# The low part of 33 weights: from a VectorE subtraction to a ScalarE negation and an adding transfer

## The chip, the core and the metric

One core of a Trainium2 chip runs the whole program. The metric is device time of one execution in microseconds. Engines are named as in the profile: PE (TensorE matmul), PEld (TensorE weight load), DVE (VectorE), ACT (ScalarE), POOL (GpSimd), SP (SyncE, which here only starts transfers).

## The reference, cut to what matters

Two blocks run one after the other on 256 latent tokens of width 1024; the first also has 256 context tokens. The first block has two layers. Each modulates its tokens, multiplies them by one wide weight matrix, and goes on in three branches: attention, a gated linear recurrence, and a spatial gating unit. Cut to the two branches that matter here:

```
h = x * (1 + scale) + shift                       # context tokens likewise
q, k, v, gates, ... = split(h @ w_in)
q, k = rope(rms_norm(q)), rope(rms_norm(k))       # 8 heads of 64, 2 key/value heads
y_attn = softmax(q @ k_all.T / 8) @ v_all * silu(a_g)
vn = layer_norm(s_v)                              # spatial gating, width 512, chunks of 128
y_sgu = s_u * (w_s @ vn + b_s) * silu(s_g)
```

In layer 0 all 512 tokens are computed; in layer 1 only the 256 latent ones need queries and gating, while keys and values are made for all 512. The second block (a gated delta rule and a convolution) isn't touched by the change.

## The kernel before, in words

All weights lie in one array W of pieces, each 128 partitions by 1024 float32 (512 KB). A product is made in three matmuls of a faster 32-bit type (F32R): each operand is split into a high part (the operand rounded to F32R) and a low part (the operand less its high part), and high x high, high x low and low x high are summed (`mm3`, L220, and `gemm_mv`, L294). A float32 product of 128 rows and up to 512 columns is thus three matmuls.

`weight` (L237) brings one piece: `raw` (L232) starts the load on SP's queue into one of three buffers tagged "raw"; then, under `urgent` (a higher place in the order of the work), `split` (L212) makes the high part `wh` with an ACT cast (L214) and the low part `wl` with a DVE subtraction (L215). `wh` and `wl` have three buffers each, so a weight can be split only when the weight three before it has been used up. The tile framework sets the order of each engine's instructions when the program is built, by priority and by the time at which it expects operands to be ready; on the chip each engine keeps to its order.

Two ways of using a weight matter here. In `gemm_mv` the weights are the moving operand, 256 columns: a pair of pieces covers the 1024 rows of the contraction, and for each tile of 128 tokens 4 steps use the first piece and then 4 steps the second, 24 matmuls per tile; a pair serves 4 tiles in layer 0 (96 matmuls) and 2 in layer 1's queries and gating values (48). In `gemm_st` (L273) one piece is the stationary operand of 8 steps, 24 matmuls of 512 columns in layer 0 and of 256 in layer 1.

`trunk` (L487) runs a layer: `attention` (L661) and then `sgu` (L553) first, each wholly, then the recurrence with the rest of the products between its steps. In layer 0 `attention` uses one piece of 512 columns (the last of four for key, value and half of the queries; the first three were used in `start`, L384) and a pair for the other queries; in layer 1 a pair for key and value and two for the queries. `sgu` uses two pairs for the values, and through `gemm_st` 4 pieces for the units (L580) and, in `gate_y` (L601), 4 for the gate. Attention's own work (softmax: DVE maxima L780, ACT exponentials L781, PE transposes and products) is laid by the framework between the products of `sgu`.

POOL's queue in this part of the program holds small loads for attention and gating (L558, L560, L666), the loads of modulation weights of `ada_sums` (L443), each of which waits for a DVE accumulation (L449) that frees its buffer, and at the start of layer 1 products on POOL itself (L1130, L1131).

Of the kernel before, what the change touches and what calls it, by code (L numbers as in the profile page):

```python
# [8 lines left out]
F32 = mybir.dt.float32  # L9
# [4 lines left out]
ALU = mybir.AluOpType  # L14
# [88 lines left out]
INDEX = {k: i for i, k in enumerate(PLAN)}  # L103
# [77 lines left out]
class Builder:  # L181
    def __init__(self, nc, tc, io):
        self.nc, self.tc, self.io = nc, tc, io
        self.n = 0
        self.hold = {}

    def nm(self, s):
        self.n += 1
        return f"{s}_{self.n}"
# [47 lines left out]
    def weight(self, key, pool=None, name="", calm=False):  # L237

        hold = self.hold.pop(key, ())
        with nullcontext(), self.behind(*hold):  # L240
            raw = self.raw(key)
        with self.urgent(), self.behind(*hold):
            h = self.t(pool or self.wpool, [P, 1024], F32R, tag="wh" + name)
            l = self.t(pool or self.wpool, [P, 1024], F32R, tag="wl" + name)
            self.split(h, l, raw)
        return h, l

    def rstd(self, pool, out, x, n):
# [238 lines left out]
    def trunk(self, l):  # L487
        nc, tc, io = self.nc, self.tc, self.io
        self.T0, self.TN = (0, 512) if l == 0 else (256, 256)
        self.tiles = [0, 1, 2, 3] if l == 0 else [2, 3]  # L490
        TN = self.TN
        with tc.tile_pool(name=f"m{l}", bufs=1) as mp:
            self.mp = mp
            if l == 0:
                self.yraw_a = self.big([P, 4, TN], tag="ya")
                self.yraw_g = self.big([P, 4, TN], tag="yg")
                self.m = [self.big([P, 4, TN], tag=f"m{i}") for i in range(2)]
            else:
                m = self.big([P, 8, TN], tag="m0")
                self.m = [m[:, 0:4], m[:, 4:8]]  # L500
                y = self.big([P, 8, TN], tag="m1")
                self.yraw_a, self.yraw_g = y[:, 0:4], y[:, 4:8]
            self.decay = self.decay_inputs(l)
            next(self.decay, None)
            with tc.tile_pool(name=f"sgu{l}", bufs=1) as sp:
                self.attention(l)
                self.sgu(l, sp)
            self.tgp = mp
            units = self.units(l)
            pre0, rate0, mid, rate1 = PACES[l]  # L510
            for n, rate, hp in ((pre0, rate0, 0), (mid, rate1, 1)):
                for _ in range(int(n)):
                    next(units, None)
                due = 0.0
                for _ in self.gla(l, hp):
                    due += rate
                    while due >= 1:
                        due -= 1
                        next(units, None)
                if l == 0 and hp == 0:  # L520
                    with tc.tile_pool(name="ada", bufs=2, side="right", reuse_waits="tile") as raws:
                        self.adaln(mp, raws)
                    self.tgp = tc.alloc_tile_pool(name="tg", bufs=1, side="right", reuse_waits="tile")
            for _ in units:
                pass
            if l == 0:
                self.g0 = self.big([P, 2, D])
                self.g1 = self.big([P, D], tag="ya")
                self.ada_gate(self.grow, [self.g0[:, 0], self.g0[:, 1], self.g1])
            for _ in self.gate_y(l, G_G, self.yraw_g):  # L530
                pass
            with tc.tile_pool(name=f"late{l}", bufs=1, reuse_waits="tile") as lp:
                self.lp = lp
                self.mh = self.t(lp, [P, 8, TN], F32R, tag="mh")
                self.ml = self.t(lp, [P, 8, TN], F32R, tag="ml")
                for _ in self.branch(l, "bg", M_G, 2, tg=self.tg):
                    pass
                if l:
                    self.out_ln(l)
                else:  # L540
                    self.tgp.release()
                    with tc.tile_pool(name="ln", bufs=1, reuse_waits="tile") as self.lp:
                        self.out_ln(l)
# [1359 lines left out]
```

## Time and profile before

| what | value |
|---|---|
| median of 3 runs | 1443.71 us (1441.45 to 1444.53) |
| the profiled execution's own time | 1437.33 us |
| its span, first to last instruction | 1435.6 us |
| layer 0's attention and gating | from about 49 to about 200 us of the span |
| layer 1's attention and gating | from about 595 to about 710 us of the span |
| mean DMA rate over the span | 131 GB/s |

The span and the rows below are of one profiled execution. A row of the view by stretch gives for each engine its busy time and, in brackets, its instructions, then the granted PE clock as a share of full speed, the mean busy share of the core's 16 DMA engines and their rate. In the views by instruction a bracket at the end tells how long the engine was idle before it and what ended that.

### The profile page before, as it was taken

To read this page: it belongs to the slowest core of one execution; us is meant where nothing else is said; L and a number is where in the kernel's file an instruction comes from. 1 tells how busy PE (TensorE), PEld (TensorE's weight loads), DVE (VectorE), ACT (ScalarE), POOL (GpSimd) and SP (SyncE) were. 2 spreads that over 40 slices of the span, in tenths; PEclk is the share of its full clock that TensorE was granted. 3 is DMA by queue.
4 is the path that set the end of the run, shared out by engine and by line. 5 is a ranking of instruction groups with operands and counts; after the bars stand their busy time and mean duration, and the time that the engine had idled before them with its cause. 6 is when DMAs were issued, how large, how long until landed. Compare 5 with 4: busy or idle time off the path is not lost.

```text
span 1435.6 us, 31593 instructions
## 1 busy us (share of the span) xinstructions
PE 1357.7 (95%) x13036; PEld 1199.8 (84%) x13036; DVE 1065.3 (74%) x2034; ACT 831.3 (58%) x1490; POOL 88.9 (6%) x260
## 2 busy tenths in 40 slices
PE   7899999999999999899999998979899999999998
PEld 4796778777877779896899988979789998989997
DVE  2598742898888268878639468877998776899785
ACT  2445533752455334656667485479685557877654
POOL 0100000111101000300001001011000000100000
PEclk9999999999999999999999999989999999999999
DMA  9442122335632236352233344424333553423362
GB/s 382 164 132 91 34 74 89 103 105 170 229 116 75 74 110 202 105 178 76 91 129 130 125 133 162 171 88 135 104 114 124 176 163 118 133 92 120 117 208 86
DMA packets 52848, 187.56 MB, mean 131 GB/s; under 512 B 6136, under 2 KB 7468, under 8 KB 52704
## 3 DMA queue, kind: packets, MB, share of 16 engines
q1 hardware_dynamic: 44640, 159.90, 33.0%
q0 software_dynamic: 6912, 24.39, 5.1%
q8 instruction: 102, 1.67, 0.5%
q10 hardware_dynamic: 1152, 1.25, 0.3%
q14 instruction: 42, 0.34, 0.1%
HBM read 184.47 MB, written 1.05 MB: 129 GB/s over the span
## 4 chain that ended last, share of the span: by engine, by line
PE 59%; DVE 15%; ACT 11%; DMA 8%; issue 5%; POOL 1%; ACTq 0%; SPq 0%; DVEq 0%; POOLq 0%
PE pg L218 47%; PE px L218 5%; DVE wl L215 4%; DMA adaw<-in_W 3%; PE px L227 3%; ACT wh L214 3%; DVE u L1761 3%; DMA raw<-in_W 2%; PE px L804 1%; DMA araw<-in_W 1%; DVE acc L449 1%; DMA xT<-in_xT 1%; DVE hTl L215 1%; PE px L987 1%; PE px L954 1%
## 5 line engine op out<-in xcount | busy, mean ns | idle before, releaser
L215 DVE TENSOR_TENSOR wl<-raw,wh 128x1024 fp32r<-128x1024 f32 x276 | 336.9, 1224 | 173.3 <-ACT wh L214 163.5
L214 ACT CAST wh<-raw 128x1024 fp32r<-128x1024 f32 (+1 forms) x278 | 289.0, 1043 | 291.6 <-PE pg L218 239.6
L218 PE MATMUL pg<-hTh,wh 128*128 128x256 f32 (+1 forms) x1440 | 454.9, 316 | 0.6 <-ACT wh L214 0.4
L218 PE MATMUL pg<-hTl,wh 128*128 128x256 f32 (+1 forms) x1440 | 449.5, 313 | 2.6 <-DVE ss L718 1.4
L218 PE MATMUL pg<-hTh,wl 128*128 128x256 f32 (+1 forms) x1424 | 444.4, 312 | 0.9 <-DVE wl L215 0.8
L218 PEld LDWEIGHTS pg<-hTl,wh 128*128 128x128 f32 x1440 | 270.6, 188 | 21.0 <-issue 5.5
L218 PEld LDWEIGHTS pg<-hTh,wh 128*128 128x128 f32 x1440 | 270.8, 188 | 20.5 <-issue 3.0
L218 PEld LDWEIGHTS pg<-hTh,wl 128*128 128x128 f32 x1424 | 268.5, 189 | 16.7 <-issue 1.4
L1761 DVE SCALAR_TENSOR_TENSOR u<-cpad,cols,u 128x256 f32<-128x256 f32 x240 | 104.8, 482 | 0.9
L218 PE MATMUL pg<-big,wh 128*128 128x512 f32 (+1 forms) x384 | 99.3, 347 | 5.5 <-DVE th L612 3.0
L218 PE MATMUL pg<-wl,hTh 128*128 128x256 f32 x320 | 91.2, 285 | 1.9 <-DVE wl L215 1.9
L218 PE MATMUL pg<-wh,hTh 128*128 128x256 f32 x320 | 91.7, 287 | 0.6 <-ACT kd L855 0.6
L218 PE MATMUL pg<-wh,hTl 128*128 128x256 f32 x320 | 91.0, 284 | 0.0
L218 PEld LDWEIGHTS pg<-big,wh 128*128 128x128 f32 x384 | 66.5, 193 | 15.5 <-DVE th L612 3.6
L218 PE MATMUL pg<-wh,mh 128*128 128x256 f32 x272 | 76.8, 284 | 0.5 <-DVE y L1320 0.5
L218 PE MATMUL pg<-wl,mh 128*128 128x256 f32 x272 | 76.7, 283 | 0.5 <-DVE wl L215 0.5
L218 PE MATMUL pg<-wh,ml 128*128 128x256 f32 x272 | 76.7, 282 | 0.0
L449 DVE SCALAR_TENSOR_TENSOR acc<-adaw,sc,acc 128x1024 f32<-128x1024 f32 x49 | 62.2, 1281 | 16.0 <-DMA adaw<-in_W 15.9
L218 PE MATMUL pg<-big,wl 128*128 128x512 f32 (+1 forms) x192 | 66.2, 346 | 0.0
L218 PEld LDWEIGHTS pg<-wl,hTh 128*128 128x128 f32 x320 | 61.1, 191 | 2.5 <-DVE wl L215 2.1
L218 PEld LDWEIGHTS pg<-wh,hTh 128*128 128x128 f32 x320 | 61.2, 191 | 1.6 <-ACT kd L855 1.0
L218 PEld LDWEIGHTS pg<-wh,hTl 128*128 128x128 f32 x320 | 61.3, 191 | 0.1
(451 smaller groups left out, 2440.4 us busy)
## 6 DMA issues: line engine op xcount, KB each, us to landing
raw<-in_W SPq DMA_DIRECT2D x282, 512.0 KB, 3.4
adaw<-in_W POOLq DMA_DIRECT2D x32, 512.0 KB, 3.6
araw<-in_W SPq DMA_DIRECT2D x16, 512.0 KB, 9.0
xT<-in_xT SPq DMA_DIRECT2D x4, 512.0 KB, 9.5
yg<-in_xtok POOLq DMA_DIRECT2D x2, 512.0 KB, 4.3
m<-in_xtok POOLq DMA_DIRECT2D x2, 512.0 KB, 5.3
nwrow<-in_nwrow POOLq DMA_DIRECT2D x2, 512.0 KB, 3.7
wsT<-in_sguw POOLq DMA_DIRECT2D x2, 256.0 KB, 3.7
```

The lines of the kernel that those rows point to most:

```text
L214: self.nc.scalar.copy(h, src)
L215: self.nc.vector.tensor_tensor(l, src, h.bitcast(F32), ALU.subtract)
L218: self.last_mm = self.nc.tensor.matmul(out, lhsT, rhs, start=start, stop=stop).ins
L227: self.nc.tensor.transpose(out, in_, self.ident[:k, :k])
L449: nc.vector.scalar_tensor_tensor(acc[:, v], raw, sc, acc[:, v], ALU.mult, ALU.add)
L804: nc.tensor.matmul(pv[64 * j:64 * j + 64, :256], kv[kt][:, 128 + 64 * g:192 + 64 * g], pTs[b][:, j * 256:(j + 1) * 256], start=kt == 0, st ...
L954: nc.tensor.matmul(out[o, a, :], x[:, a, o], y[:, a, o], start=True, stop=True, tile_position=(0, 32 * b))
L987: nc.tensor.matmul(pa[ks, a, ts], e[ch, li, a, ks], qe[ch, li, a, ts], start=True, stop=True, tile_position=(64 * d, s0))
L1761: nc.vector.scalar_tensor_tensor(out, src, w, out, ALU.mult, ALU.add)
```

## The change

A flag, `relief`, is on while `attention` and `sgu` of each layer are laid out. While it is on, `weight` makes the low part in another way: ACT casts the high part as before; ACT then writes its negative into the low part's tile; and a second transfer of the same piece of W, started by POOL (`gpsimd.dma_start` with an adding `accum_op`), adds the weight itself, so that the tile holds weight less high part. The DVE subtraction falls away for these weights. The raw load on SP's queue stays, and its buffer is now read by the cast alone.

```diff
@@ -183,6 +183,7 @@
         self.nc, self.tc, self.io = nc, tc, io
         self.n = 0
         self.hold = {}
+        self.relief = False
 
     def nm(self, s):
         self.n += 1
@@ -242,7 +243,13 @@
         with self.urgent(), self.behind(*hold):
             h = self.t(pool or self.wpool, [P, 1024], F32R, tag="wh" + name)
             l = self.t(pool or self.wpool, [P, 1024], F32R, tag="wl" + name)
-            self.split(h, l, raw)
+            if self.relief:
+
+                self.nc.scalar.copy(h, raw)
+                self.nc.scalar.mul(l, h.bitcast(F32), -1.0)
+                self.nc.gpsimd.dma_start(l, self.io["W"][INDEX[key]], accum_op=ALU.add)
+            else:
+                self.split(h, l, raw)
         return h, l
 
     def rstd(self, pool, out, x, n):
@@ -503,8 +510,10 @@
             self.decay = self.decay_inputs(l)
             next(self.decay, None)
             with tc.tile_pool(name=f"sgu{l}", bufs=1) as sp:
+                self.relief = True
                 self.attention(l)
                 self.sgu(l, sp)
+                self.relief = False
             self.tgp = mp
             units = self.units(l)
             pre0, rate0, mid, rate1 = PACES[l]
```

## Rows read from the trace of the kernel before

**Rows 1.** The page: busy time of each engine, and the two costliest groups.
```profile
PE 1357.7 (95%) x13036; PEld 1199.8 (84%) x13036; DVE 1065.3 (74%) x2034; ACT 831.3 (58%) x1490; POOL 88.9 (6%) x260
...
L215 DVE TENSOR_TENSOR wl<-raw,wh 128x1024 fp32r<-128x1024 f32 x276 | 336.9, 1224 | 173.3 <-ACT wh L214 163.5
L214 ACT CAST wh<-raw 128x1024 fp32r<-128x1024 f32 (+1 forms) x278 | 289.0, 1043 | 291.6 <-PE pg L218 239.6
```
**Rows 2.** Busy time by stretch: layer 0, then layer 1; clock, DMA share, GB/s last.
```profile
40.00:100.00 60.00, 55.69 (x413) 49.17 (x406) 43.59 (x83) 25.94 (x48) 4.43 (x8) 0.97 0.44 144
100.00:150.00 50.00, 49.65 (x272) 35.79 (x271) 44.20 (x99) 29.62 (x80) 2.14 (x4) 1.00 0.27 88
150.00:200.00 50.00, 49.43 (x265) 34.24 (x264) 34.04 (x59) 28.55 (x65) 0.61 (x2) 1.00 0.14 45
...
590.00:607.80 17.80, 14.12 (x120) 13.62 (x118) 16.60 (x30) 10.72 (x24) 10.51 (x6) 1.00 0.26 88
613.50:637.20 23.70, 23.38 (x197) 23.07 (x196) 17.45 (x34) 13.05 (x20) 0.00 (x0) 1.00 0.54 177
637.20:649.00 11.80, 11.80 (x97) 11.27 (x97) 11.59 (x29) 6.80 (x14) 0.00 (x0) 1.00 0.57 182
```
**Rows 3.** Waits of PE: one row of 40 to 270 us, three of 590 to 665.
```profile
PE pg L218 <- DVE wl L215: 1.9, 1, 1.9
...
PE px L227 <- DVE yg L1100: 2.3, 1, 2.3
PE pg L218 <- DVE th L595: 1.9, 1, 1.9
PE pg L218 <- DVE ss L718: 1.4, 1, 1.4
```
**Rows 4.** Timeline of DVE at the end of layer 0: start, duration, instruction.
```profile
592.19 1.23 DVE L215 TENSOR_TENSOR wl<-raw,wh 128x1024 fp32r<-128x1024 f32 x1
...
593.67 1.22 DVE L215 TENSOR_TENSOR wl<-raw,wh 128x1024 fp32r<-128x1024 f32 x1
```
**Rows 5.** Timeline of ACT in layer 1's query products: three casts.
```profile
617.84 1.05 ACT L214 CAST wh<-raw 128x1024 fp32r<-128x1024 f32 x1 [0.93 <-PE pg L218]
619.26 1.05 ACT L214 CAST wh<-raw 128x1024 fp32r<-128x1024 f32 x1 [0.38 <-PE pg L218]
...
623.54 1.05 ACT L214 CAST wh<-raw 128x1024 fp32r<-128x1024 f32 x1 [0.16 <-PE pg L218]
```
**Rows 6.** Timeline of DVE there: the subtraction after the cast at 617.84.
```profile
618.92 1.23 DVE L215 TENSOR_TENSOR wl<-raw,wh 128x1024 fp32r<-128x1024 f32 x1 [3.04 <-ACT wh L214]
```
**Rows 7.** Timeline of PE, start of layer 0's attention: first and seventh of seven matmuls.
```profile
50.93 0.50 PE L218 MATMUL px<-wh,hTh 128*128 128x512 f32 x1 [2.15 <-ACT wh L214]
...
52.75 0.50 PE L218 MATMUL px<-wl,hTh 128*128 128x512 f32 x1 [0.18 <-DVE wl L215]
```
**Rows 8.** Queues SP (q1) and POOL (q0): packets, MB, share; landings of the modulation weights' loads.
```profile
q1 hardware_dynamic: 44640, 159.90, 33.0%
q0 software_dynamic: 6912, 24.39, 5.1%
...
DMA to landing us min/median/max: 2.1/3.6/5.7
```
**Rows 9.** The chain that ended last, layer 0 after attention: start, duration, matmuls.
```profile
195.56 36.93 PE pg L218 x158
```
**Rows 10.** Busy time by stretch around the wait of 1.9 us; the clock is third from last.
```profile
70.00:72.10 2.10, 0.23 (x3) 0.03 (x1) 2.10 (x3) 0.58 (x1) 0.00 (x0) 1.00 0.00 0
72.10:75.00 2.90, 2.88 (x17) 2.88 (x18) 2.90 (x3) 0.37 (x1) 0.00 (x0) 0.67 0.64 209
75.00:78.00 3.00, 3.00 (x21) 3.00 (x21) 2.65 (x14) 0.00 (x1) 0.53 (x1) 0.75 0.82 225
```
**Rows 11.** Timeline of POOL: a load in layer 0, a product at layer 1's start.
```profile
91.47 0.53 POOL L443 DMA_DIRECT2D adaw<-in_W  x1 [15.52 <-DVE acc L449]
...
594.36 2.78 POOL L1130 TENSOR_TENSOR yg<-yg,big 128x1024 f32<-128x1024 f32 x1
```

## The prediction

> **What bounds the kernel now.** I read the page's first part, then busy time by stretch, then what TensorE (PE) waited for, then the timelines of single engines. PE is busy for 95% of the span; the DVE subtraction that makes a weight's low part is the costliest DVE group, 276 times 1.224 us, and the ACT cast ahead of it takes 1.04 us [rows 1]. That looks like relief wanted. The stretches of attention and gating say otherwise: in layer 0 DVE is busy for 44.20 of 50 us at one point, yet PE for 49.65 of the same 50; in layer 1's run of plain products PE is busy for 23.38 of 23.70 and 11.80 of 11.80 us [rows 2]. PE is the bound there, and DVE works beside it. What PE waits for from DVE is small: in layer 0 one wait of 1.9 us for a low part, in layer 1 waits of 2.3, 1.9 and 1.4 us for other DVE results [rows 3]. So the change can gain only a few microseconds, and the question is what it does to the moment at which a low part is ready.
>
> **The change, part by part.** It touches 33 weights: 15 in layer 0 (one of the 512-wide key, 2 of queries, 4 of the gating values, 8 of the gating units) and 18 in layer 1 (2 key/value, 4 query, 12 gating). Each loses one DVE subtraction, 33 x 1.224 = 40.4 us of DVE; gains one ACT multiplication of the same 128x1024 shape, 33 x 1.04 = 34.3 us of ACT; and gains a 512 KB transfer on POOL's queue that adds into the tile.
>
> *The DVE time* lies beside PE except at the waits named. Two of the subtractions stand in DVE's queue straight ahead of the last normalization of layer 0 [rows 4], for which PE then waits 2.3 us. I take 3 us of gain: that wait and a little of the others; the ends are 0 and 1.9 + 2.3 + 1.9 + 1.4 = 7.5.
>
> *The ACT time.* ACT is busy for 29.62 of 50, 28.55 of 50 and 13.05 of 23.7 us [rows 2], so the cover is its idle time. In attention the softmax's ACT steps are in the same queue: without cover the 14 gating-unit weights cast there x 1.04 = 14.6 us, but each 1.22 us less on DVE is on the same chain. I take 0.
>
> *When a low part is ready.* This is the main term. The weight pool has three buffers. In layer 1 a query or value product uses a pair of weights for 48 matmuls; 197 matmuls in 23.70 us are 0.120 us each, so a pair lasts 5.7 us, and casts indeed come 5.70 us apart [rows 2, 5]. The second weight of a pair takes the buffer of the first weight of the pair before, which comes free 12 matmuls ahead of that pair's end. Take the cast at 617.84: the other weight of the running pair comes free at its end, about 619.2 [rows 5]. PE needs the low part 14 matmuls after that end, at 619.2 + 1.7 = 620.9. Today it is there at 618.92 + 1.23 = 620.15 [rows 6], 0.75 us to spare. After the change: cast and multiplication end at 617.84 + 2 x 1.05 = 619.94, and then comes the transfer's landing time T. So T would have to be under 1.0 us. PE's order can help: only 8 of the 48 matmuls need this low part, so with all 40 others ahead of them it is needed at 619.2 + 4.8 = 624.0, and T may be 4.1. The order in the program does so where a low part was planned late: at 50.93 six matmuls with the high part run ahead of the first with the low part [rows 7].
>
> No accumulating transfer is in the trace. The nearest are the plain 512 KB loads on POOL's queue: 2.1, 3.6, 5.7 us from issue to landing (least, median, longest) [rows 8]. Bounds: 2.1, since more is done than in a plain load, and 7.2, two medians. I take 5.7, the longest plain one, since the transfer runs beside the raw loads and also has to read the tile that it adds to. Then the low part is late by 619.94 + 5.7 - 624.0 = 1.6 us with the best order and by 4.7 with today's; I take 2.2, near the best order. Such second weights: four in layer 1 (the key pair ahead of them has room while PE waits for the layer's input) and three in layer 0, 7 x 2.2 = 15.4 us, less the wait of 1.9 us of that kind that is there now [rows 3]: **+13.5**.
>
> *The first weight of layer 0's attention* ends its cast as PE starts on it at 50.9, after a wait of 2.15 us [rows 7]. Its 16 high-part matmuls, at 36.93 / 158 = 0.234 us for 512 columns [rows 9], last until 54.6; the low part comes at 50.9 + 1.05 + 5.7 = 57.6. Up to 3 late; **+2**.
>
> *Gating units.* A weight's buffer comes free two weights before its use. In layer 0 that is 2 x 24 x 0.234 = 11.2 us against 2.1 + 5.7 = 7.8: nothing. In layer 1 it is 2 x 24 x 0.120 = 5.8, up to 7.7 with high parts first: 0 to 2 per round of three, I take 0.5 for each of the first four: **+2**.
>
> *PE's clock.* After the wait at 70.2 the granted clock is 0.67 and 0.75 for the next 5.9 us, so partly 1.2 GHz instead of 2.4, against 1.00 before; that loses 0.33 x 2.9 + 0.25 x 3 = 1.7 us [rows 10]. Not every short wait does this: after the 2.3 us wait in layer 1 it stayed at 1.00 [rows 2]. I count two such drops more than now: **+3.4** (0 to 7 x 1.7 = 12).
>
> *POOL's queue* is in order. The loads of the modulation weights wait in it for DVE, up to 15.52 us, and in layer 1 a 2.78 us product stands in it beside the first key weights [rows 11]. An adding transfer behind one of them waits too, with PE behind it. DVE is freer then, and layer 0's gating units have 3.4 us to spare: I take 0, and keep 15 as the end.
>
> Sum: 13.5 + 2 + 2 + 3.4 - 3 = +18 us. The profiled execution took 1437.3 us (span 1435.6), 6.4 below the median of the runs shown, 1443.7; it becomes 1455, and the median 1461 to 1462.
>
> *The 16 DMA engines.* 24.39 MB on POOL's queue took 5.1% of 1435.6 us, 3.0 us per MB, so 1.57 us for one weight, about as on SP's [rows 8]. In layer 1's products the raw loads alone keep the engines busy for 0.54 of the time [rows 2]; a second plain load makes 1.08, just over full: another reason to put T at the long end.
>
> The plain loads' landings of 3.6 us in the median and 5.7 at most [rows 8] can be held against a rule. The Trainium skill ("DMA: Bandwidth & Descriptors", "Anatomy of one DMA — SWDGE (gpsimd) path") fits a transfer from this queue as some 2.0 us and its bytes over 436 GB/s, 3.2 us here as an estimate; by that, with the best order, pairs and start would cost nothing and the sum would be about -3. The rows are longer already for a plain load, so they decide. The same page ("Rules for kernel authors") says that an accumulating transfer reads its destination and writes it later, which speaks for more; no run here shows what that costs.
>
> **Rivals.**
> *The transfers become the bound (slower still).* If the adding transfer costs the engines double, 3.15 us, the 12 weights between 613.5 and 649.0 need 12 x (1.55 + 3.15) = 56 us against 35.5: +21. With T = 7.2 the three pairs of layer 0 are late by 3.1 to 6.2, say 4.5 each, 13.5 - 1.9 = +11.6; the start +4.5, three clock drops +5: +42, 1486; some POOL waits bring 1495. For it: 1.08. Against: the other stretches are at 0.14 to 0.57 [rows 2].
> *Covered, and DVE's relief counts (faster).* If T stays under 4.1 us and PE's order has all high-part matmuls in front, no low part is late. The median plain landing, 3.6, meets that. Then the gain on DVE's waits remains, 3 to 7.5 us: 1436 to 1441, say 1438. Its place is the second weight of the layer 1 pairs; T = 4.1 decides. Against it: today's order at those pairs has the low part in its turn, and landings beside raw loads run longer.
> *Covered with nothing gained (no change).* The same with lateness and gain cancelling: 1443.
>
> **How the numbers follow.** Forecast 0.55, its own range 1449 to 1475 (lateness 1 to 3.5 us per pair, clock 0 to 7); transfers as the bound 0.22; faster 0.13; no change 0.10. About 0.2%, 2.9 us, is what a measurement of this kernel can tell from none. Range 1438 to 1495: it leaves out half of the faster case and the worst of the POOL waits. Faster 0.13, same 0.10, slower 0.77.
>
> **What would show it.** Right: in layer 1's products PE waits for POOL's transfer or DMA at second weights, a few us each, casts further apart than 5.7 us, granted clock under 1 there, PE idle up by some 15 us, DVE busy down by 40. Landing near 5.7. Wrong: landing under 4 and PE still dense from 613 to 649 (faster or same); DMA share near 1 through that stretch and casts 9 us apart (second rival); or PE waiting behind a modulation load on POOL's queue.

## The result and the profile after

| kernel | median | ratio, 95% interval |
|---|---|---|
| before | 1444.12 us | |
| after | 1504.78 us (1503.48 to 1508.09, 4 runs) | 1.0428 [1.0407, 1.0449] |

Slower, as forecast, but by 60.7 us where some 18 were forecast, and beyond the range's end of 1495. The page of after: its first part, the two queues, the subtraction's group and the new transfer with its median landing (last number). Lines of the shared helpers stand one further on than before (the matmul's L218 is L219, the yg product's L1100 L1109); the changed weights' cast is L248, their negation L249, their transfer L250.

```profile
span 1503.3 us, 31635 instructions
...
PE 1378.4 (92%) x13036; PEld 1221.0 (81%) x13036; DVE 1034.7 (69%) x2001; ACT 861.6 (57%) x1523; POOL 116.7 (8%) x293
...
q1 hardware_dynamic: 44640, 159.90, 31.8%
q0 software_dynamic: 11664, 41.69, 11.5%
...
L216 DVE TENSOR_TENSOR wl<-raw,wh 128x1024 fp32r<-128x1024 f32 x243 | 296.7, 1223 | 165.9 <-ACT wh L215 155.4
...
wl<-in_W POOLq DMA_DIRECT2D x33, 512.0 KB, 7.7
```

Against [rows 1, 8]: 33 subtractions are gone (276 to 243, 40.2 us of DVE), ACT is busy for 30 us more, POOL's queue moves 17.3 MB more. PE runs the same 13036 matmuls in 1378.4 us instead of 1357.7, and outside them its idle time went from 1435.6 - 1357.7 = 77.9 to 1503.3 - 1378.4 = 124.9 us. So the 67.7 us between the two spans are **47.0 of idle and 20.7 of slower matmuls**. The view of PE's waits of after (us in all, times, longest):

```profile
PE pg L219 <- DMA wl<-in_W: 32.9, 11, 7.3
PE px L228 <- DVE xs L1250: 11.4, 2, 8.9
PE px L219 <- DMA wl<-in_W: 8.0, 1, 8.0
...
PE px L228 <- DVE yg L1109: 5.1, 1, 5.1
```

The new transfer is waited for 12 times, 40.9 us; the wait for xs is the same 11.4 us in before. The matmul with the low part of the first weight is one (8.0); three more stand in layer 0 (15.9) and eight in layer 1 (17.0). The page parts them by use: the gating units, where the weight is the stationary operand, waited 10.4 us for the transfer, the pairs, where it is the moving one, 22.5 (last number).

```profile
L219 PE MATMUL pg<-hTh,wl 128*128 128x256 f32 (+1 forms) x1424 | 446.8, 314 | 12.9 <-DMA wl<-in_W 10.4
...
L219 PE MATMUL pg<-wl,hTh 128*128 128x256 f32 x320 | 95.7, 304 | 22.5 <-DMA wl<-in_W 22.5
```

By stretch, with the columns of [rows 2]: the start of layer 0's attention, and layer 1's products.

```profile
44.00:54.00 10.00, 7.75 (x29) 5.00 (x27) 3.67 (x16) 7.55 (x10) 3.20 (x5) 0.86 0.46 132
54.00:62.00 8.00, 0.00 (x0) 0.00 (x0) 1.42 (x2) 1.04 (x2) 2.28 (x3) 0.71 1.02 273
62.00:68.00 6.00, 5.98 (x24) 4.99 (x25) 0.00 (x0) 2.51 (x4) 0.00 (x0) 0.76 0.95 254
...
655.00:665.00 10.00, 7.93 (x44) 7.73 (x43) 0.00 (x0) 2.47 (x3) 1.47 (x2) 0.69 1.02 225
665.00:675.00 10.00, 7.84 (x61) 7.43 (x61) 0.82 (x1) 7.19 (x11) 1.71 (x2) 0.97 0.79 192
675.00:685.00 10.00, 6.07 (x38) 5.86 (x37) 9.44 (x30) 3.86 (x7) 1.72 (x2) 0.72 1.03 229
```

From 54 to 62 us PE does nothing while the DMA engines are full (1.02). In layer 1, where PE was dense at clock 1.00 with the engines at 0.54 and 0.57 [rows 2], it now does 38 to 61 matmuls in 10 us instead of some 83, the engines are full in two of the three stretches (from 645.7 to 700 us their mean is 0.89), and the granted clock drops to 0.69 and 0.72.

To place the loss, three marks cut a span: the first product of a recurrence step in layer 0 (which follows attention and gating), the first transpose of layer 1's input, and the recurrence's first product in layer 1. The first and third are the first of the two times in a row of tile paT (one row for each half of the span), the second that in a row of tile m. First the kernel before:

```profile
L218 PE MATMUL px<-a,paT x16: 377/379/379, 250.2 to 390.4; 65*128 65x256 f32 x16
L218 PE MATMUL px<-a,paT x16: 377/378/380, 716.0 to 830.0; 65*128 65x256 f32 x16
L227 PE MATMUL px<-ident,m x16: 271/272/273, 579.3 to 580.9; 128*128 128x128 f32 x16
```
The same three of after:
```profile
L219 PE MATMUL px<-a,paT x16: 377/379/379, 278.3 to 424.6; 65*128 65x256 f32 x16
L219 PE MATMUL px<-a,paT x16: 377/378/380, 777.3 to 891.5; 65*128 65x256 f32 x16
L228 PE MATMUL px<-ident,m x16: 272/272/273, 613.0 to 614.6; 128*128 128x128 f32 x16
```

Layer 0 up to its mark lost 28.1 us, layer 1 (third mark less second) 164.3 - 136.7 = 27.6. The stretch between, 5.6, and the end, 6.4, hold none of the changed weights: the profiled execution of before was at the fast end of its runs, and two controls below show the like there. Their layer 1 takes 137.6 and 142.4, so what the change costs there is some 22 to 27. Each kernel was profiled once, so a few us between two marks say little.

### The profile page after: what moved, and what is told of

The parts are those of the page before. It is cut to its first block, busy times and chain, and to the rows that moved or that the text cites. A ratio compares the mean times of both kernels' runs of the same rounds, so it can differ in the third digit from the quotient of the medians.

```text
span 1503.3 us, 31635 instructions
## 1 busy us (share of the span) xinstructions
PE 1378.4 (92%) x13036; PEld 1221.0 (81%) x13036; DVE 1034.7 (69%) x2001; ACT 861.6 (57%) x1523; POOL 116.7 (8%) x293
## 3 DMA queue, kind: packets, MB, share of 16 engines
q0 software_dynamic: 11664, 41.69, 11.5%
HBM read 201.77 MB, written 1.05 MB: 135 GB/s over the span
## 4 chain that ended last, share of the span: by engine, by line
PE 53%; DVE 13%; ACT 11%; DMA 9%; issue 8%; POOL 1%; ACTq 0%; POOLq 0%; DVEq 0%; SPq 0%
PE pg L219 42%; PE px L219 5%; DMA adaw<-in_W 4%; DVE wl L216 3%; DMA wl<-in_W 3%; ACT wh L215 3%; DMA raw<-in_W 3%; PE px L228 3%; DVE u L1770 2%; PE px L813 1%; PE px L1583 1%; PE px L963 1%; PE px L996 1%; ACT L1497 1%; DVE acc L456 0%
## 5 line engine op out<-in xcount | busy, mean ns | idle before, releaser
L219 PE MATMUL pg<-hTh,wh 128*128 128x256 f32 (+1 forms) x1440 | 458.3, 319 | 2.0 <-ACT qkv L698 0.9
L219 PE MATMUL pg<-hTh,wl 128*128 128x256 f32 (+1 forms) x1424 | 446.8, 314 | 12.9 <-DMA wl<-in_W 10.4
L219 PE MATMUL pg<-hTl,wh 128*128 128x256 f32 (+1 forms) x1440 | 450.3, 313 | 0.6 <-issue 0.6
L216 DVE TENSOR_TENSOR wl<-raw,wh 128x1024 fp32r<-128x1024 f32 x243 | 296.7, 1223 | 165.9 <-ACT wh L215 155.4
L215 ACT CAST wh<-raw 128x1024 fp32r<-128x1024 f32 (+1 forms) x245 | 254.7, 1042 | 269.1 <-PE pg L219 215.6
L219 PEld LDWEIGHTS pg<-hTh,wl 128*128 128x128 f32 x1424 | 270.6, 190 | 30.6 <-DMA wl<-in_W 11.2
L219 PEld LDWEIGHTS pg<-hTh,wh 128*128 128x128 f32 x1440 | 273.0, 190 | 22.1 <-issue 3.4
L219 PEld LDWEIGHTS pg<-hTl,wh 128*128 128x128 f32 x1440 | 272.9, 189 | 16.9 <-issue 2.9
L219 PE MATMUL pg<-wl,hTh 128*128 128x256 f32 x320 | 95.7, 304 | 22.5 <-DMA wl<-in_W 22.5
L219 PE MATMUL pg<-big,wh 128*128 128x512 f32 (+1 forms) x384 | 100.5, 350 | 4.6 <-DVE th L621 3.0
L219 PE MATMUL pg<-wh,hTh 128*128 128x256 f32 x320 | 95.8, 300 | 0.6 <-ACT kd L864 0.6
L219 PE MATMUL pg<-wh,hTl 128*128 128x256 f32 x320 | 95.1, 298 | 0.0
L219 PEld LDWEIGHTS pg<-wl,hTh 128*128 128x128 f32 x320 | 65.0, 206 | 25.6 <-DMA wl<-in_W 24.0
L219 PEld LDWEIGHTS pg<-big,wh 128*128 128x128 f32 x384 | 67.4, 195 | 14.9 <-DVE th L621 3.6
L219 PE MATMUL pg<-wl,mh 128*128 128x256 f32 x272 | 76.7, 283 | 0.6 <-DVE wl L216 0.6
L219 PE MATMUL pg<-wh,mh 128*128 128x256 f32 x272 | 76.7, 283 | 0.4 <-DVE y L1329 0.3
L219 PE MATMUL pg<-wh,ml 128*128 128x256 f32 x272 | 76.6, 282 | 0.0
L219 PEld LDWEIGHTS pg<-wh,hTh 128*128 128x128 f32 x320 | 65.8, 206 | 1.2 <-ACT kd L864 1.0
L219 PE MATMUL pg<-big,wl 128*128 128x512 f32 (+1 forms) x192 | 66.7, 348 | 0.0
L219 PEld LDWEIGHTS pg<-wh,hTl 128*128 128x128 f32 x320 | 65.8, 206 | 0.2
```

The source lines that it names most:

```text
L215: self.nc.scalar.copy(h, src)
L216: self.nc.vector.tensor_tensor(l, src, h.bitcast(F32), ALU.subtract)
L219: self.last_mm = self.nc.tensor.matmul(out, lhsT, rhs, start=start, stop=stop).ins
```

## The experiments

"L0" is the first mark, "layer 1" the third less the second, "landing" the new transfer from issue to landing (least, median, longest), "waits" PE's for it, in all.

| run | median us | ratio, 95% interval | L0 | layer 1 | landing | waits |
|---|---|---|---|---|---|---|
| before | 1444.1 | | 250.2 | 136.7 | | |
| after | 1504.8 | 1.043 [1.041, 1.045] | 278.3 | 164.3 | 5.3/7.7/13.0 | 40.9 |
| negate_then_dve | 1443.8 | 1.001 [0.999, 1.002] | 248.8 | 142.4 | | |
| plain_transfer | 1478.1 | 1.024 [1.021, 1.027] | 267.1 | 155.7 | 3.4/5.6/8.4 | 27.8 |
| buffers_4 | 1470.2 | 1.018 [1.015, 1.022] | 257.6 | 156.7 | 5.4/7.8/11.6 | 22.9 |
| low_last | 1481.5 | 1.027 [1.025, 1.028] | 263.2 | 159.2 | 5.2/7.3/12.4 | 29.7 |
| pairs_only | 1486.7 | 1.030 [1.027, 1.034] | 269.1 | 157.8 | 5.5/8.1/12.3 | 29.0 |
| units_only | 1458.6 | 1.011 [1.008, 1.014] | 251.1 | 145.0 | 5.3/7.1/8.8 | 5.7 |
| mods_on_sp | 1490.2 | 1.033 [1.029, 1.036] | 274.6 | 163.1 | 5.3/7.9/12.9 | 39.0 |
| before_low_last | 1445.0 | 1.001 [1.000, 1.003] | 248.4 | 137.6 | | |
| low_last_buffers_4 | 1466.4 | 1.014 [1.010, 1.018] | 253.2 | 152.5 | 5.5/8.6/11.9 | 19.6 |
| layer0_units | 1449.5 | 1.004 [1.001, 1.006] | 252.2 | 138.1 | 5.9/6.7/9.0 | 0 |
| from_sbuf | 1486.4 | 1.029 [1.026, 1.032] | 265.6 | 163.1 | 4.4/5.9/9.5 | 30.2 |
| before_mods_on_sp | 1436.8 | 0.995 [0.993, 0.997] | 246.2 | 137.8 | | |

**1. The ACT step alone.** ACT casts and negates; DVE adds the weight; no second transfer.
```diff
-                self.nc.gpsimd.dma_start(l, self.io["W"][INDEX[key]], accum_op=ALU.add)
+                self.nc.vector.tensor_tensor(l, l.bitcast(F32), raw, ALU.add)
```


> The negation on ACT stays, the transfer goes, and DVE adds the raw weight to the negated high part instead. Late landing, or full DMA engines, or POOL's queue: all three lie in the transfer, so 1441 to 1452 us, the low part being 1 us later than before. ACT: the 33 extra ACT operations cost most of the loss, 1470 us or more.

Measured: 1443.77 us, 1.0006 [0.9989, 1.0023]. ACT 863.1 us busy, as in after, and PE 1363.2; DVE has as much to do as before (1065.1). The 33 more ACT operations and their wait cost nothing that can be measured; the whole loss comes with the transfer.

**2. The same transfer without adding.**
```diff
-                self.nc.gpsimd.dma_start(l, self.io["W"][INDEX[key]], accum_op=ALU.add)
+                self.nc.gpsimd.dma_start(l, self.io["W"][INDEX[key]])
```


> The second transfer loses its adding, so the low part's tile ends up holding the weight itself: the output leaves out the subtraction of the high part. Order and waits stay. Late landing (the adding transfer lands 7.7 us after its issue, a plain one some 4 to 5): PE's waits for the low part's tile shrink from 41 us to 10 to 20, the granted clock drops less often, 1455 to 1475 us. ACT (the extra multiplication delays attention) or POOL's queue (modulation loads ahead of the transfers): neither changes, 1495 to 1505 us.

Measured: 1478.13 us, +34: between the two forecasts, with waits of 27.8 us where 10 to 20 were expected. The line of POOL's queue on its page (packets, MB, share):
```profile
q0 software_dynamic: 11664, 41.69, 8.6%
```
Already a plain second transfer costs over half of the loss, and adding the other 27 us. Even plain, it lands in 5.6 us at these places, against 3.6 for the plain loads of before [rows 8]. The engines' time follows from the queue's share, less the queue's 5.1% of before: plain (8.6% x 1480.6 - 5.1% x 1435.6) / 33 = 1.6 us for a weight, adding (11.5% x 1503.3 - 73.2) / 33 = **3.0 us**: twice as much, for the same bytes in the queue's row. This run's layer 1 products by stretch:
```profile
640.00:650.00 10.00, 6.58 (x41) 6.38 (x42) 0.00 (x0) 4.70 (x6) 1.58 (x3) 0.84 0.91 306
650.00:660.00 10.00, 9.33 (x78) 9.13 (x77) 1.37 (x2) 7.81 (x11) 1.06 (x2) 0.98 0.59 173
660.00:670.00 10.00, 5.91 (x32) 5.70 (x30) 9.13 (x31) 3.83 (x7) 1.05 (x2) 0.70 0.76 257
670.00:680.00 10.00, 9.71 (x78) 9.35 (x76) 4.34 (x18) 7.64 (x14) 1.58 (x3) 0.96 0.61 187
```
The engines are full in none of these stretches (inside them at 1.09 from 646 to 649 and 1.05 from 663 to 666 us), and still layer 1 takes 155.7 us, 13 to 19 more than in before and the controls, with 12.4 us of waits for the transfer. So the larger part of layer 1's loss does not need engines that are full all through.

**3. A fourth buffer for the split weights.** Every fourth weight of attention and gating goes into a pool of its own.
```diff
+            if self.xp_ is not None:
+                if self.turn % 4 >= 3:
+                    pool = self.xp_
+                self.turn += 1
...
-            with tc.tile_pool(name=f"sgu{l}", bufs=1) as sp:
+            with tc.tile_pool(name=f"sgu{l}", bufs=1) as sp, tc.tile_pool(name=f"wx{l}", bufs=1) as wx:
+                self.xp_, self.turn = wx, 0
```


> The changed kernel with a fourth buffer for high and low parts while attention and gating are laid out. Late landing against the buffer's return: the second weight of a pair now has a whole pair's time more, 5.7 us in layer 1 and 11.3 in layer 0, against some 10 us from buffer to low part; layer 0's three waits of 7.3, 4.4 and 4.2 us go, the 8 us at its start stay, layer 1's shrink: 1455 to 1475 us. Full DMA engines: layer 0 gains, but layer 1's run of products stays at 50 us or more with a DMA share of 0.9 or more: 1475 to 1485 us.

Measured: 1470.18 us; layer 0 gets back 20.7 of its 28.1 us, layer 1 only 7.6. The total lies in the range of late landing. PE's waits in layer 0 behind the first weight fall from 15.9 to 0.9 us, those in layer 1 only from 17.0 to 15.5. So in layer 0 the loss is mostly what the prediction called lateness: a landing too long for the time between a buffer's return and the low part's use. Its layer 1 by stretch:
```profile
645.00:655.00 10.00, 5.11 (x40) 4.70 (x40) 5.33 (x19) 5.80 (x8) 2.57 (x3) 1.00 1.02 241
655.00:665.00 10.00, 9.38 (x79) 9.17 (x78) 4.35 (x12) 6.35 (x10) 1.72 (x2) 1.00 1.01 247
665.00:675.00 10.00, 7.34 (x58) 6.71 (x56) 6.70 (x24) 9.28 (x17) 2.74 (x4) 1.00 1.03 268
675.00:690.00 15.00, 12.89 (x79) 11.64 (x79) 6.62 (x15) 10.55 (x18) 2.44 (x3) 0.89 1.05 266
```
With a buffer more the transfers start sooner, and for 45 us on end the DMA engines are full, 1.01 to 1.05, while PE is busy for 34.71 of 45 and waits for the transfer for 8.7. There the full engines are the likely limit; ahead of it, from 625 to 645 us, they are at 0.81.

**4. All matmuls with the low weight last**, per output tile of a pair. 20 matmuls then stand ahead of the second weight's low part instead of 14; the prediction's "best order" had all 40 others of a layer 1 pair ahead of it, and no run has that.
```diff
-                self.mm(out, sh, rl, False, k == KT - 1)
+            for k in range(KT):
+                l = w[k // 4][1]
+                self.mm(out, ah[:, k, i * P:(i + 1) * P], l[:, (k % 4) * 256:(k % 4 + 1) * 256], False, k == KT - 1)
```


> The changed kernel with the products of pairs reordered: for each tile all matmuls with high parts first, the 8 with low parts last. Late landing: the low part of a pair's second weight may come 1 us later in each tile, so 4 to 7 us less per layer in waits and a few clock drops less: 1485 to 1497 us. Full DMA engines: layer 1's products take as long as before the reordering, 54 us, and only layer 0 gains: 1495 to 1503 us.

The same edit on the kernel before, as a control:

> The kernel before, with the products of pairs reordered so that the 8 matmuls with low parts come last in each tile. It removes at most the one wait of 1.9 us for a low part and its clock drop, in any theory: 1438 to 1445 us. If it were 10 us faster or more, the gain of the reordering in the changed kernel would not be due to the late transfer.

Measured: 1481.49 us, 23 less than after; the control 1445.02, no change. That is more than either forecast gave. Even this first part of the order that the prediction had leaned on was thus worth 23 us, and the program had not made it.

**5. Only the pairs, or only the units.** The condition `self.relief` is narrowed to `key[0] != "st"` (17 weights) or `key[0] == "st"` (16).

> Only the 17 moving-operand weights (queries, keys, values, gating values and the first 512-wide one) get the changed low part; the 16 stationary ones of the gating units and gate are split as before. Late landing against the buffer's return: the pairs have 3.1 us from buffer to use and carry most of the loss: 1480 to 1497 us. A cost per weight (DMA work, ACT, POOL's queue): about half of the loss, 1470 to 1478 us.

> Only the 16 stationary weights of gating units and gate get the changed low part. Late landing against the buffer's return: layer 0's have 11.2 us and lose nothing, layer 1's first four have 5.8 us against 10 and lose some 4 us in a round of three, with a clock drop or two: 1446 to 1458 us. A cost per weight: about half of the loss, 1470 to 1478 us.

Measured: +42.6 and +14.5 us against before's 1444.1; together 57, nearly the whole 60.7. The pairs lie in the range of late landing, the units 0.6 us above it. In layer 0 the units cost 0.9 us at the mark, the pairs 18.9; some 8 of layer 0's 28.1 us come only with both. In after one gating unit of layer 0 waits for its low part, in neither of these two runs does one.

**6. Only layer 0's units**, 8 weights for which neither a late low part nor full engines were foreseen.
```diff
-            if self.relief:
+            if self.relief and key[0] == "st" and key[2] == 0:
```


> Only the 8 stationary weights of layer 0's gating units and gate get the changed low part. They have 11.2 us or more from buffer to use. Late landing against the buffer's return: no wait, 1440 to 1447 us, no measurable gain either since PE is the bound there. DVE's relief: some 10 us of DVE time less in attention, 1432 to 1438 us. A cost per weight: 8 x 1.8 us, 1458 us.

Measured: 1449.46 us, 1.0036 [1.0014, 1.0058], which none of the three forecasts gave. PE waits for no transfer, though one lands in 6.7 us, and the relief of DVE (1057.5 us busy, 8 less) still gains nothing: it is 5 us slower. Where those go is not settled: the L0 mark is 2.0 later, the rest is spread beyond it.

**7. POOL's queue.** The modulation weights' loads move to SP, in after and in before.
```diff
-            nc.gpsimd.dma_start(raw, self.io["W"][INDEX["ada", l, part, k]])
+            nc.sync.dma_start(raw, self.io["W"][INDEX["ada", l, part, k]])
```


> The changed kernel with the 32 loads of modulation weights moved from POOL's queue to SP's, so that no adding transfer stands behind one that waits for DVE. Late landing: the trace shows one adding transfer held up so, by 1.9 us, so little changes: 1495 to 1508 us. POOL's queue: layer 0's waits shrink by 10 us or more, 1485 to 1494 us.

> The kernel before with the 32 loads of modulation weights on SP's queue. In the changed kernel this move took 15 us off. If that was POOL's queue ahead of the adding transfers, the kernel before, which has none, stays within 4 us of 1443.5; if it is a gain of its own (the loads come earlier for the layer's later part), it falls to 1430 to 1438 us.

Measured: after gains 14.5 us, where I had expected no change; but before gains some 7 as well. PE's waits for the transfer stay at 39.0, and of after's gain only 3.7 lies ahead of the L0 mark (before: 4.0) and 1.2 in layer 1; the rest lies where no adding transfer is under way. Transfers held up in POOL's queue are therefore not what costs the 60 us. The total lies where the forecast for POOL's queue put it, but without that forecast's sign, shorter waits. POOL's timeline of after shows the place in layer 0 where an adding transfer was held up, 1.9 us behind its negation's end at 78.87:
```profile
80.26 0.54 POOL L450 DMA_DIRECT2D adaw<-in_W  x1 [7.30 <-DVE acc L456]
80.79 0.91 POOL L250 DMA_DIRECT2D wl<-in_W  x1
```
A second one, at the start of layer 1, waited 1.4 us (629.43 to 630.82) behind a product on POOL; PE waited for neither key weight. before_mods_on_sp, 1436.76 us, **beats both kernels**: DVE's waits for these loads at L449 fall from 15.9 to 7.0 us.

**8. Both remedies together**, the fourth buffer and the low parts last.

> The changed kernel with the fourth buffer and with low parts last. Late landing alone: either remedy took 23 to 35 us off; together the low parts are in time nearly everywhere, layer 0 is left with its start and layer 1's attention and gating falls to some 145 us from modulation to the recurrence's first product (164 in the changed kernel, 142 where DVE makes the sum): 1450 to 1458 us. Full DMA engines in layer 1: that stretch stays at 153 us or more with the share at 1.0: 1460 to 1468 us.

Measured: 1466.37 us. Layer 0 is back to 253.2, 3 us from before. Layer 1 stays at 152.5, and again, by stretch, the engines are full:
```profile
645.00:655.00 10.00, 9.23 (x78) 9.03 (x76) 5.50 (x20) 8.98 (x14) 3.14 (x4) 1.00 1.00 239
655.00:665.00 10.00, 8.03 (x54) 7.87 (x54) 6.13 (x18) 4.83 (x7) 1.28 (x3) 0.83 1.04 280
665.00:675.00 10.00, 8.03 (x63) 7.47 (x63) 3.90 (x16) 7.73 (x15) 2.50 (x3) 1.00 1.03 233
```
But only 4.7 of layer 1's 14.7 us of waits for the transfer lie in these 30 us; from 615 to 645 the engines are at 0.75.

**9. A shorter landing with the same adding.** The transfer adds from the loaded tile instead of from W in HBM.
```diff
-                self.nc.gpsimd.dma_start(l, self.io["W"][INDEX[key]], accum_op=ALU.add)
+                self.nc.gpsimd.dma_start(l, raw, accum_op=ALU.add)
```


> The adding transfer reads the weight from the raw tile already on the chip, not again from HBM. If its landing and its load on the DMA engines come from the adding itself: 7 to 8 us landing and 1495 to 1510 us as before. If they come from reading HBM a second time: landing under 6 us and 1475 to 1485 us. The raw buffers are held longer, which can cost some us.

Measured: 1486.38 us, 1.4 above the second forecast, whose landing came true and whose lighter engines did not. POOL's queue on its page:
```profile
q0 software_dynamic: 11664, 41.69, 11.1%
```
The landing is 1.8 us shorter and the engines' time nearly the same, (11.1% x 1485.3 - 73.2) / 33 = 2.8 us for a weight. Layer 0 gains 12.7 us, layer 1 1.2. Layer 0 thus follows the landing. Layer 1 by stretch, then two rows of its waits:
```profile
640.00:650.00 10.00, 6.57 (x44) 6.37 (x43) 0.00 (x0) 4.32 (x6) 0.86 (x1) 0.83 1.06 243
650.00:660.00 10.00, 6.36 (x44) 5.95 (x44) 3.16 (x11) 6.42 (x9) 2.57 (x3) 0.87 0.90 217
660.00:670.00 10.00, 8.96 (x58) 8.54 (x56) 7.35 (x22) 5.15 (x8) 1.21 (x2) 0.79 0.81 202
...
SPq L235 <- DMA wl<-raw: 106.3, 18, 17.3
...
ACT wh L248 <- DMA raw<-in_W: 9.8, 3, 5.2
```
This run does not show that layer 1 follows the engines' load instead, since they are full in one of the three stretches only. The edit has a price of its own there: a raw buffer comes free only when the adding transfer has read it, so SP's loads stand behind these transfers (106.3 us), and in layer 1 ACT's casts wait 9.8 us for raw weights, which they do not in after.

## Why the prediction was wrong

**Right:** PE is the bound and DVE's relief is worth next to nothing (run 6, for 8 of the weights); the ACT step at 0 (run 1); the loss comes at low parts that land late, at the clock and at the DMA engines. The sign follows from these. What failed are the sizes of the sum's terms:

| term | forecast, us | after |
|---|---|---|
| pairs, less the 1.9 of before | +13.5 | 22.5 - 1.9 = +20.6 |
| first weight of layer 0 | +2 | +8.0 |
| gating units | +2 | +10.4 |
| PE's clock (slower matmuls) | +3.4 | +15.2 to +20.7 |
| DVE's relief (the wait for yg) | -3 | 5.1 - 2.3 = +2.8 |
| sum | +18 | +57 to +62.5 |

The medians differ by 60.7. The steps one by one:

*"I take 5.7, the longest plain one."* The landing measured 5.3, 7.7 and 13.0 us. The median is above even the end that was kept, 7.2. The plain landings were read from loads that ran beside less: in layer 0's attention and gating the engines were at 0.14 to 0.44 [rows 2]. Here the transfer runs beside raw loads (1.02 from 54 to 62 us) and is itself the heavier one. The fit of the Trainium skill ("DMA: Bandwidth & Descriptors", "Anatomy of one DMA — SWDGE (gpsimd) path") gives 3.2 us as an estimate; the runs show 5.6 for a plain transfer here and 7.7 for an adding one, so it does not hold for either. What the Trainium skill says of an accumulate on the same page ("Rules for kernel authors"), that it reads its destination and writes it later, fits the doubled engine time, 3.0 against 1.6 us; no run shows that this is the reason.

*"I take 2.2, near the best order."* The row with six high-part matmuls ahead [rows 7] stands at a layer's first weight; at the pairs the program left each low part in its turn, with one or two exceptions. PE's timeline of after in layer 1:
```profile
658.92 0.28 PE L219 MATMUL pg<-wh,hTh 128*128 128x256 f32 x1
659.04 0.28 PE L219 MATMUL pg<-wh,hTl 128*128 128x256 f32 x1
661.39 0.39 PE L219 MATMUL pg<-wl,hTh 128*128 128x256 f32 x1 [2.07 <-DMA wl<-in_W]
661.61 0.28 PE L219 MATMUL pg<-wh,hTh 128*128 128x256 f32 x1
```
With today's order the step's own sum gives 7 x 4.7 - 1.9 = 31 us for the forecast's landing, and for the measured one 4.7 + 2.0 = 6.7 us for a second weight and 45 in all, where I wrote 13.5. PE waited 20.6 us more at the pairs than before. So the order was taken too well, and the sum with today's order is too high; that a late pair also gives the next one more time is a possible reason, which no run tests.

*"+2" for the first weight.* PE waited 8.0 us: its transfer was issued at 51.6 us and PE went on at 62.02, 10.4 later where the step had 5.7, with the engines full from 54 on.

*"I count two such drops more than now" (+3.4).* The same matmuls took 20.7 us more of PE's time; against run 1, whose weights wait for no transfer, 15.2. Both are above the end that the step kept, 12. The drops follow the waits, in after's timeline:
```profile
88.90 0.58 PE L219 MATMUL pg<-wl,hTh 128*128 128x256 f32 x1 [7.34 <-DMA wl<-in_W]
89.28 0.41 PE L219 MATMUL pg<-wh,hTh 128*128 128x256 f32 x1
...
88.90:90.50 1.60, 1.60 (x7) 1.60 (x8) 1.46 (x5) 0.00 (x0) 0.44 (x1) 0.50 1.04 218
```
A 256-column matmul starts every 0.21 us there, against 0.12 at the full clock of 2.4 GHz [rows 2]; the last row, of the view by stretch, has the granted clock at 0.50, the lower level of 1.2 GHz. Twelve waits in place of one gave not two drops but stretches at 0.69 to 0.86. What the clock alone costs was not run by itself.

*"Transfers become the bound", put at 0.22, not in the forecast.* Its condition, double engine time (3.15 us), held at 3.0, and its +21 for layer 1 is close to the 22 to 27 that layer 1 lost. But that closeness is not shown to be more than luck: the plain transfer of run 2 costs layer 1 already 13 to 19 us with the engines at 0.59 to 0.91, and in after their mean there is 0.89. The 1.08 that the prediction had for a plain second transfer held for the pace of before; at the slower pace of run 2 the mean of its four stretches is 0.72. The sum of that rival, 1486, allowed layer 0 11.6 + 4.5 us ahead of the clock, and layer 0 lost 28. The Trainium skill ("DMA: Bandwidth & Descriptors", "Issuing engines are not separate DMA queues") says that transfers started by different engines run on the same 16 DMA engines and interleave; the rows agree: 1.02 in the stretch from 54 to 62, with both queues loading. Runs 3 and 8 show the engines full for 30 to 45 us, 1.00 to 1.05, once the lateness is relieved, and 10 to 20 us of loss left in layer 1. How much of layer 1's loss is the landing and how much the engines' load stays open: no run took their load alone away, and the landing was itself longer where the load was fuller (3.6 us for the plain loads of before, 5.6 for the plain transfer of run 2).

Of the small terms, the DVE gain of 3 us did not come: PE's wait for yg, which it was to shorten, grew from 2.3 [rows 3] to 5.1 us. POOL's queue at 0 was right but for the two cases of 1.9 and 1.4 us.

The gating units, +2, made PE wait 10.4 us, 6.2 of them in layer 1. The other 4.2 stand in layer 0, where the step had nothing:
```profile
132.06 0.79 PE L219 MATMUL pg<-hTh,wl 128*128 128x512 f32 x1 [4.18 <-DMA wl<-in_W]
```
The weights of layer 0's second and third unit were cast together at 120.28 us, right behind the last pair; the second one's transfer was issued at 123.54, and PE, which began the first unit at 119.82, came to this low part some 6 us later: one weight's products, not the two (11.2 us) that the step counted on. By themselves the units cost +14.5 (run 5), of which layer 1 shows 3 to 8; the rest was not placed.

## What to carry to other kernels

Before work moves from an engine to the DMA, price two things in the stretch where it will run: the transfer's landing against the time between a buffer's return and the first use, and the sum of all transfers on the 16 engines against the stretch's length. An engine that is busy for 74% of the time but hardly waited for, as DVE here, is not worth relieving. Take the order of a queue from the rows at the place itself; a reordering seen once elsewhere is not one that the program will make again.

## What was not expected of the hardware

- An adding transfer of 512 KB takes 3.0 us of all 16 DMA engines where a plain one takes 1.6, and lands 2.1 us later in the median (7.7 against 5.6).
- Adding from SBUF instead of HBM shortens the landing to 5.9 us but hardly the engines' load (2.8 us).
- POOL is held for 0.86 us by the issue of an adding transfer, for 0.53 by that of a plain one [rows 11]; the row of tile wl on POOL in after (ns, least, median, longest):
```profile
L250 POOL DMA_DIRECT2D wl<-in_W x33: 849/862/934, 51.6 to 730.6; - x33
```
- Loads moved from POOL's queue to SP's made the kernel before faster by 0.5% (0.9948 [0.9930, 0.9966]), with the same 16.8 MB moved by one queue instead of the other.
